# A streaming encoder step on one core: the opening written out by hand for three units at once, without GpSimd arithmetic

## The chip, the cores and the metric

The kernel runs on one core of a Trainium2 chip. Its time is device microseconds of one execution; the median of several runs counts. A core has a matrix engine (PE, with its weight loads shown apart as PEld), a vector engine (DVE), an activation engine (ACT), GpSimd (POOL) and a queue engine (SP), which here issues all transfers. Each works through its own queue in order and waits on semaphores for the others.

## What is computed

One layer of a hybrid encoder, for a prompt of 1024 tokens and a sample of 32:

```python
mod = jax.nn.silu(c) @ p['w_ada'] + p['b_ada']
shift, scale, gate = jnp.split(mod, 3, axis=-1)
hn = rmsnorm(x, p['norm_g']) * (1.0 + scale[:, None]) + shift[:, None]
proj = hn @ p['w_in']
lru_x, lru_g, xbc, z, dt_raw = jnp.split(proj, [...], axis=-1)
...  # RG-LRU on lru_x, gated by lru_g
xbc_c, new_buf_ssd = causal_conv(xbc, buf_ssd, p['ssd_conv_w'], p['ssd_conv_b'])
xs, Bm, Cm = jnp.split(silu(xbc_c), [...], axis=-1)
...  # chunked SSD scan on xs, B, C and dt, gated by z, grouped rmsnorm
mix = jnp.concatenate([y_lru, y_ssd], axis=-1) @ p['w_out']
out = x + gate[:, None] * mix
```

All in float32; the model width is 1024, and w_in has 4624 columns.

## The kernel before

Features lie on the 128 partitions, tokens along the free axis. A *unit* is 128 columns of w_in: a tile of 8 k-tiles of 128x128. 36 units make the input projection; units 24 and 25 are B, 26 and 27 are C, 16 to 23 are xs, 28 to 35 are z, 0 to 15 the LRU part. Tokens come in three blocks (`BLK`): 384, 384 and 290 columns, the last with 256 prompt tokens, 32 sample tokens and 2 columns that hold the shift.

Products are taken in three passes, to keep float32 accuracy: weights and activations are each split into a high part (a cast, on ACT) and a low part (a subtraction), and hi\*hi, hi\*lo and lo\*hi are accumulated (`mm_part`, lines 219 to 221). `load_unit` fetches and splits a unit; the raw, high and low tiles have three buffers each. A unit's product with one block takes one of four PSUM banks tagged "main"; the other four serve everything small.

The shift is not added to the activations. It is multiplied as two extra columns of block 2, and `evacuate` adds the resulting two biases (`shift_bias`) when ACT copies a bank out. So a unit's first two blocks can be copied out only when its third is done.

The opening is the part that this change touches. It must

- load x in three blocks, square it, sum the squares (`load_x`), and from the sums get 1/rms per token (`sum_x`: matmul, root on ACT, reciprocal on DVE), spread it over the partitions by matmul (`spread`), and scale x (`norm_x`);
- multiply 16 units of w_ada with silu(c) (`ada_unit`, line 114; eight for the scale, eight for the shift), copy each row out (line 115), turn it into columns by matmul (`ada_columns`, line 120), and make `Acol` = norm_g * (1 + scale) for each of the 8 k-tiles (`scale_columns`);
- split the scaled x times Acol into `hb` (`h_new`: high part on ACT, line 210, low part on DVE, line 211);
- multiply units 24 and 25 and the dt columns (`dt_block`, line 266) with it.

Inside `tc.manual_schedule` the named engines take their instructions in the order of the program; on the others a planner orders them by simulated time, and it may put later work into gaps. Before, SP and PE are named. Their order comes from two strings, `XLOAD` for the loads and `PROG` for the matmul engine: W is a warm-up matmul on `ones` (line 289), a an ada unit of the scale, s one of the shift, c columns, r and R the sum and scaling of a block of x, p and q one k-tile of unit 24 and 25, d the dt block. GpSimd adds the squares of blocks 1 and 2, scales three k-tiles of block 0 and all of blocks 1 and 2 (line 194, from an SBUF copy of the spread), and makes the low part of unit 24. The opening ends with unit 24's third block; unit 25's third block follows, then units 26 and 27, in the planner's order, with their convolutions (line 419), the dt chain and the SSD loop.

Of the kernel before, what the change touches and what calls it, by code (L numbers as in the profile page):

```python
# [50 lines left out]
def encoder_step(ctx: ExitStack, tc: tile.TileContext, a, o):  # L58
# [98 lines left out]
    xs_in, xsq, xcol, Adone = {}, {}, {}, []  # L157

    def load_x(b, k0, k1):
        c0, n = XB[b]  # L160
# [4 lines left out]
        eng = nc.gpsimd if b else nc.vector
        for k in range(k0, k1, 2):
            tag = "u" if k else ("raw", "zs", "raw")[b]
            sq = cpool.tile([128, 2, 384], F32, name="xsq", tag=tag, bufs=1 if tag == "zs" else 2)[:, :, 0:n]
# [1 line left out]
            nc.scalar.activation(sq, x, AF.Square)  # L170
            if k == 0:
                xsq[b] = sq
            else:
                eng.tensor_add(xsq[b], xsq[b], sq)
        if k1 == KT:
            eng.tensor_add(xsq[b][:, 0, :], xsq[b][:, 0, :], xsq[b][:, 1, :])
# [5 lines left out]
    def norm_x(b):  # L182
        n = XB[b][1]
        bc = spread(xcol[b], n, "xbc")
        sb = cpool.tile([128, 384], F32, name="xbs", tag="raw", bufs=2)[:, 0:n]
        nc.scalar.copy(sb, bc[:, 0:n])
        k = 0
        while k < KT:
            step = 1 if b == 0 else 2
            x = xs_in[b][:, k:k + step, 0:n]  # L190
            if b == 0 and k not in POOL_K:
                nc.vector.tensor_mul(x, x, bc[:, None, 0:n].to_broadcast([128, step, n]))
            else:
                nc.gpsimd.tensor_mul(x, x, sb[:, None, :].to_broadcast([128, step, n]))
            k += step
            ready[b] = k
            h_new()

    ready = [0, 0, 0]
    hdone = [0, 0, 0]  # L200

    def h_new():
        for b in range(3):
            while hdone[b] < min(ready[b], len(Adone)):
                k = hdone[b]
                hdone[b] += 1
                x = xs_in[b][:, k, :]
                for (s, e, w) in [(0, 384, 0)] if b < 2 else [(0, 256, 0), (256, 288, 1)]:
                    hi = hb[b][:, k, 0, s:e]
                    nc.scalar.activation(hi, x[:, s:e], AF.Copy, scale=Acol[:, k, w:w + 1])  # L210
                    nc.vector.scalar_tensor_tensor(hb[b][:, k, 1, s:e], x[:, s:e], Acol[:, k, w:w + 1],  # L211
                                                   hi.bitcast(F32), op0=OP.mult, op1=OP.subtract)
# [59 lines left out]
    with tc.manual_schedule(engines={mybir.EngineType.SP, mybir.EngineType.PE}):  # L272
        dma(cT, a["cT"])
        dma(par, a["par"])
        nc.vector.memset(ones, 1.0)
# [22 lines left out]
        def scale_columns(n):
            k = len(Adone)
            pcol = ada_columns(srow[:, k * 128:(k + n) * 128], n)  # L300
            for i in range(n):
                nc.scalar.activation(Acol[:, k + i, :], pcol[:, i, :], AF.Identity, scale=pc(P_NG, k + i),
                                     bias=b1[:, k + i:k + i + 1])
            Adone.extend(range(k, k + n))
            h_new()

        wB = [None, None]
        sraw = []
        bk = [bk_b0, bk_b1]
        cnt = dict.fromkeys("acrRdpqsW", 0)  # L310
        lcnt = dict.fromkeys("sxwBC", 0)

        def load_next():
            c, n = loads[0], lcnt[loads[0]]
            if c == "s":
                if n >= SR + cnt["a"] + cnt["s"]:
                    return False
                sraw.append(st.tile([128, KT, 128], F32, name="sraw", tag="sraw", bufs=SR))
                dma(sraw[n], a["w_ada"][(n + KT) % (2 * KT)])
            elif c == "x":  # L320
                if n >= XP[0] + XP[1] and cnt["R"] < 1:
                    return False
# [709 lines left out]
```

## Time and profile before

| | |
|---|---|
| median of 3 runs | 786.5 us (785.12 to 788.98) |
| profiled execution | 786.8 us |
| its span, first to last instruction | 785.1 us |
| mean granted clock of PE | 0.987 |
| PE busy | 761.6 us, 97% |
| DVE, ACT, POOL busy | 534.5, 415.2, 78.0 us |
| moved by DMA | 96.32 MB, mean 123 GB/s |

A row of a profile in order of time reads: start in us, duration in us, engine, line, operation, output <- inputs, shapes, count (xN merges N neighbours), and in brackets the idle time of the engine ahead of it and what ended it. In such rows a matmul's duration includes a drain that overlaps the next one, so the distance between starts is its cost in a stream. A row of a stage gives its bounds, its length, and then each engine's busy time with its count, the granted clock, the share of DMA in use and GB/s.

### The profile page before, as it was taken

What the parts mean: (1) busy time and instruction counts of PE and PEld (TensorE: products, weight loads), DVE (VectorE), ACT (ScalarE), POOL (GpSimd) and SP (SyncE); (2) the same over time, 40 slices, a digit from 0 to 9 for tenths busy, and PEclk for the clock granted to TensorE, in tenths of its full rate; (3) what the DMA queues carried; (4) which work ended last, traced back from release to release, by engine and by line L of the source; (5) the groups of instructions that cost most, each with busy time, mean ns of one, the idle gap of its engine ahead of it and who ended that gap; (6) DMA issues with size and microseconds to landing.
All of it is one profiled execution on the core that took longest, in us unless ns stands there. A gap on an engine that the chain in (4) does not pass through costs nothing.

```text
span 785.1 us, 13046 instructions
## 1 busy us (share of the span) xinstructions
PE 761.6 (97%) x5230; PEld 737.0 (94%) x5230; DVE 534.5 (68%) x842; ACT 415.2 (53%) x609; POOL 78.0 (10%) x179
## 2 busy tenths in 40 slices
PE   8899999999999999999999999999999999999994
PEld 7678999989999999998999999999999999999994
DVE  3575966798887787877475566546658897635643
ACT  6553855335244253443578877886777654323430
POOL 3581211001000000000010011101101000000000
PEclk9899999999999999999999999999999999999997
DMA  9920214244433424342212111111153685744831
GB/s 326 395 101 2 78 40 139 88 134 139 137 110 121 147 63 161 116 122 89 78 66 88 43 61 35 54 34 61 31 150 114 191 276 162 236 138 142 262 111 68
DMA packets 40188, 96.32 MB, mean 123 GB/s; under 512 B 4536, under 2 KB 22208, under 8 KB 40128
## 3 DMA queue, kind: packets, MB, share of 16 engines
q1 hardware_dynamic: 40128, 95.50, 37.7%
q8 instruction: 41, 0.67, 0.3%
q14 instruction: 19, 0.16, 0.1%
HBM read 85.53 MB, written 9.95 MB: 122 GB/s over the span
## 4 chain that ended last, share of the span: by engine, by line
PE 80%; DVE 9%; DMA 5%; ACT 2%; issue 2%; POOL 1%; SPq 0%; POOLq 0%; DVEq 0%; ACTq 0%
PE pj L221 16%; PE pj L219 16%; PE pj L220 16%; PE mix L862 6%; PE mix L860 6%; PE mix L861 6%; PE yd L608 2%; PE dS L583 2%; DVE hb L211 2%; DMA M<-dA_d 2%; DVE wlo L97 1%; DMA sraw<-in_w_ada_dram 1%; PE yo L623 1%; DVE M L551 1%; PE gt L744 1%
## 5 line engine op out<-in xcount | busy, mean ns | idle before, releaser
L220 PE MATMUL pj<-hb,whi 128*128 128x384 f32 (+1 forms) x864 | 282.8, 327 | 2.5 <-DVE hb L211 2.5
L219 PE MATMUL pj<-hb,whi 128*128 128x384 f32 (+1 forms) x864 | 284.6, 329 | 0.0
L221 PE MATMUL pj<-hb,wlo 128*128 128x384 f32 (+1 forms) x864 | 282.4, 327 | 1.2 <-POOL wlo L97 1.2
L220 PEld LDWEIGHTS pj<-hb,whi 128*128 128x128 f32 x864 | 163.3, 189 | 4.2 <-DVE hb L211 3.2
L221 PEld LDWEIGHTS pj<-hb,wlo 128*128 128x128 f32 x864 | 163.6, 189 | 3.1 <-POOL wlo L97 1.6
L219 PEld LDWEIGHTS pj<-hb,whi 128*128 128x128 f32 x864 | 162.7, 188 | 3.2 <-issue 2.9
L95 ACT CAST whi<-wraw 128x1024 fp32r<-128x1024 f32 x84 | 88.0, 1048 | 142.3 <-PE pj L220 69.4
L97 DVE TENSOR_TENSOR wlo<-wraw,whi 128x1024 fp32r<-128x1024 f32 x83 | 102.5, 1236 | 59.3 <-ACT whi L95 59.3
L862 PE MATMUL mix<-yt,wlo 128*128 128x324 f32 (+2 forms) x320 | 103.9, 326 | 1.0 <-DVE wlo L97 1.0
L860 PE MATMUL mix<-yt,whi 128*128 128x324 f32 (+2 forms) x320 | 104.1, 325 | 0.0
L861 PE MATMUL mix<-yt,whi 128*128 128x324 f32 (+2 forms) x320 | 103.7, 324 | 0.0
L419 DVE SCALAR_TENSOR_TENSOR u<-raw,par,u 128x1060 f32<-128x1060 f32 x60 | 79.7, 1328 | 1.6 <-ACT u L417 1.1
L862 PEld LDWEIGHTS mix<-yt,wlo 128*128 128x128 f32 x320 | 60.0, 188 | 1.4 <-DVE wlo L97 1.3
L860 PEld LDWEIGHTS mix<-yt,whi 128*128 128x128 f32 x320 | 60.1, 188 | 0.2
L861 PEld LDWEIGHTS mix<-yt,whi 128*128 128x128 f32 x320 | 60.0, 188 | 0.1
L238 ACT ACTIVATE raw<-pj,sb 128x384 f32<-128x384 f32 (+2 forms) x80 | 33.9, 477 | 23.0 <-PE pj L221 13.3
L551 DVE TENSOR_TENSOR_SCAN M<-M,mask 128x1060 f32<-128x1060 f32 x16 | 37.8, 2363 | 11.8 <-DMA M<-dA_d 11.8
L879 DVE SCALAR_TENSOR_TENSOR ot<-mix,gate,xr 128x352 f32<-128x352 f32 (+3 forms) x32 | 14.8, 489 | 25.4 <-PE mix L862 21.5
L405 POOL COPY cso<-raw 128x3 f32<-128x3 f32 x20 | 11.8, 590 | 195.9 <-ACT raw L238 195.9
L211 DVE SCALAR_TENSOR_TENSOR hb<-x,Acol,hb 128x384 fp32r<-128x384 f32 (+2 forms) x32 | 28.0, 925 | 3.8 <-ACT hb L210 3.8
L756 DVE SCALAR_TENSOR_TENSOR r<-a,r 128x1060 f32<-128x1060 f32 x8 | 10.1, 1264 | 28.2 <-ACT r L755 28.2
L554 ACT ACTIVATE M<-M 128x1060 f32<-128x1060 f32 x16 | 17.5, 1091 | 22.2 <-DVE M L551 20.3
(228 smaller groups left out, 1063.5 us busy)
## 6 DMA issues: line engine op xcount, KB each, us to landing
wraw<-in_w_out_dram SPq DMA_DIRECT2D x48, 512.0 KB, 3.6
wraw<-in_w_in_dram SPq DMA_DIRECT2D x36, 512.0 KB, 3.7
M<-dA_d SPq DMA_DIRECT2D x16, 530.0 KB, 4.9
sraw<-in_w_ada_dram SPq DMA_DIRECT2D x16, 512.0 KB, 10.2
E<-E_d SPq DMA_DIRECT2D x16, 265.0 KB, 4.0
yz_d<-y SPq DMA_DIRECT2D x8, 530.0 KB, 4.2
wraw<-in_w_ada_dram SPq DMA_DIRECT2D x8, 512.0 KB, 4.4
x<-in_xh_dram SPq DMA_DIRECT2D x4, 384.0 KB, 4.8
```

The lines of the kernel that those rows point to most:

```text
L95: nc.scalar.copy(hi, raw)
L97: eng.tensor_sub(lo, raw, hi.bitcast(F32))
L211: nc.vector.scalar_tensor_tensor(hb[b][:, k, 1, s:e], x[:, s:e], Acol[:, k, w:w + 1], hi.bitcast(F32), op0=OP.mult, op1=OP.subtract)
L219: nc.tensor.matmul(out, lhsT=hi[:, kk, :], rhs=hh, start=(kk == 0), stop=False)
L220: nc.tensor.matmul(out, lhsT=hi[:, kk, :], rhs=hl, start=False, stop=False)
L221: nc.tensor.matmul(out, lhsT=lo[:, kk, :], rhs=hh, start=False, stop=(kk == KT - 1))
L238: nc.scalar.activation(dst[0:P, off + d:off + d + e - s], banks[b][0:P, s:e], func, bias=sb[0:P, w:w + 1])
L419: nc.vector.scalar_tensor_tensor(u, raw[:, k:k + TW], wcol(k), u, op0=OP.mult, op1=OP.add)
L551: nc.vector.tensor_tensor_scan(M, M, mask, 0.0, op0=OP.add, op1=OP.mult)
L860: nc.tensor.matmul(ps, lhsT=w[0][:, k, :], rhs=yh, start=(half == 1 and k == 0), stop=False)
L861: nc.tensor.matmul(ps, lhsT=w[0][:, k, :], rhs=yl, start=False, stop=False)
L862: nc.tensor.matmul(ps, lhsT=w[1][:, k, :], rhs=yh, start=False, stop=(half == 0 and k == KT - 1))
```

## The change

- PE, SP, ACT, DVE and POOL all follow the written order in the opening; the strings are gone.
- Three units (24, 25, 26) are multiplied k-tile by k-tile: for each k-tile first hi\*hi and lo\*hi of each unit, then hi\*lo of each.
- Loads: x block 0, then w24, s0, w25, s1, s2, w26, s3, s4, x block 1 (halves around s5); each further ada unit is issued after the one whose buffer it takes; x block 2 comes after block 0 is done, in a buffer that it shares with it.
- GpSimd only sets, copies three columns at a time and saves; sums, scalings and weight splits go to DVE. DVE also makes Acol, and ACT copies all ada rows.
- The first two blocks of the three units are copied out without the shift ("parked") into raw tiles, and DVE adds the bias to these 768 columns once block 2 is there.
- Behind the opening, B of group 0 is processed first, then unit 27 is multiplied; dt block 2 stands after block 2 of the units.

```diff
-        eng = nc.gpsimd if b else nc.vector
...
+    def square_x(b, k):
+        n = XB[b][1]
+        if k == 0:
+            xsq[b] = st.tile([128, 2, 384], F32, name="xacc", tag="xacc", bufs=2)[:, :, 0:n]
+        sq = xsq[b] if k == 0 else cpool.tile([128, 2, 384], F32, name="xsq", tag="u", bufs=2)[:, :, 0:n]
+        nc.scalar.activation(sq, xin[b][:, k:k + 2, :], AF.Square)
+        if k:
+            nc.vector.tensor_add(xsq[b], xsq[b], sq)
+        if k == KT - 2:
+            nc.vector.tensor_add(xsq[b][:, 0, :], xsq[b][:, 0, :], xsq[b][:, 1, :])
...
+    def scale_x(b, k, n=1):
+        w = XB[b][1]
+        x = xin[b][:, k:k + n, :]
+        nc.vector.tensor_mul(x, x, xbc[b][:, None, 0:w].to_broadcast([128, n, w]))
...
-    with tc.manual_schedule(engines={mybir.EngineType.SP, mybir.EngineType.PE}):
+    with tc.manual_schedule(engines={E.SP, E.PE, E.Activation, E.DVE, E.Pool}):
...
+        def ada_scale(k):
+            pcol = ada_columns(srow[:, k * 128:(k + 1) * 128], 1)
+            nc.vector.scalar_tensor_tensor(Acol[:, k, :], pcol[:, 0, :], pc(P_NG, k),
+                                           b1[:, k:k + 1].to_broadcast([128, 2]), op0=OP.mult, op1=OP.add)
...
+        def mm_k(us, b, k):
+            for u in us:
+                mm_head(u, b, k)
+            for u in us:
+                mm_tail(u, b, k)
...
+        def park(u, b):
+            if u not in raws:
+                raws[u] = raw_tile(FIRST[u] - 8, ssd_state(FIRST[u] - 16), ("raw", "raw", "zs")[u])
+            for (s, e, d, w) in EV[b]:
+                nc.scalar.copy(raws[u][:, 3 + d:3 + d + e - s], banks[u][b][:, s:e])
...
+        split_w(0)
+        warm(9)
+        sum_x(0)
+        ada_row(0, srow)
+        load_s()
+        warm(3)
+        spread_x(0)
+        ada_scale(0)
+        split_w(1)
+        ada_row(1, srow)
+        load_s()
+        scale_x(0, 0)
+        split_h(0, 0)
...
+        square_x(1, 0)
+        mm_k((2,), 0, 2)
+        mm_k((2,), 0, 3)
+        mm_k((0, 1, 2), 0, 4)
+        ada_row(5, srow)
+        load_s()
+        square_x(1, 2)
+        warm(4)
+        ada_scale(5)
+        split_h(0, 5)
+        square_x(1, 4)
+        mm_k((0, 1, 2), 0, 5)
+        ada_row(6, srow)
+        square_x(1, 6)
+        ada_scale(6)
+        split_h(0, 6)
+        sum_x(1)
+        ada_row(7, srow)
+        spread_x(1)
+        ada_scale(7)
+        split_h(0, 7)
+        scale_x(1, 0, 2)
+        mm_k((0, 1, 2), 0, 6)
+        split_h(1, 0)
+        mm_k((0, 1, 2), 0, 7)
+        load_x(2, 0, 4)
...
+        for k in range(KT):
+            if k % 2 == 0 and k < 6:
+                scale_x(1, k + 2, 2)
+            if k < 6:
+                split_h(1, k + 2)
+            mm_k((0, 1, 2), 1, k)
+            ada_row(KT + k, hrow)
...
+            if k >= 4:
+                square_x(2, 2 * (k - 4))
+        for u in range(3):
+            park(u, 1)
+        dt_block(0)
+        sum_x(2)
+        dt_block(1)
+        spread_x(2)
         pcol = ada_columns(hrow, 8)
         nc.vector.tensor_add(shift, pcol, ...)
...
+        for k in range(0, KT, 2):
+            scale_x(2, k, 2)
+            split_h(2, k)
+            split_h(2, k + 1)
+        for k in range(KT):
+            mm_k((0, 1, 2), 2, k)
+        sbs = []
+        for u in range(3):
+            sbs.append(shift_bias(banks[u]))
+            evacuate(raws[u], 3, AF.Identity, banks[u], 128, (2,), sbs[u])
+            r = raws[u][:, 3:771]
+            nc.vector.tensor_scalar(r, r, sbs[u][:, 0:1], None, op0=OP.add)
+            save_raw(raws[u], FIRST[u] - 8)
         pd = dt_block(2)
...
+    b_post(0, raws[0])
+    banks = project(load_unit(a["w_in"][27]))
+    b_post(1, raws[1])
     dt_chain()
-    for g in range(2):
-        w = load_unit(a["w_in"][26 + g])
-        c_post(g, project(w))
+    c_post(0, raws[2])
+    c_post(1, ssd_raw(banks, 11))
```

More of the change, by code (lines that the diff above doesn't have):

```diff
@@ L156, in encoder_step @@
     XB = ((0, 384), (384, 384), (768, 288))
-    xs_in, xsq, xcol, Adone = {}, {}, {}, []
+    xin, xsq, xcol, xbc = {}, {}, {}, {}
     def load_x(b, k0, k1):
@@ L180, in sum_x, with spread_x, split_h @@
         token_rstd(xcol[b], xsq[b][:, 0, :], XB[b][1], "xcol")
[L182 to L212, printed above, removed]
+    def spread_x(b):
+        xbc[b] = spread(xcol[b], XB[b][1], "xbc")
+    def scale_x(b, k, n=1):
+        w = XB[b][1]
+        x = xin[b][:, k:k + n, :]
+        nc.vector.tensor_mul(x, x, xbc[b][:, None, 0:w].to_broadcast([128, n, w]))
+    def split_h(b, k):
+        x = xin[b][:, k, :]
+        for (s, e, w) in [(0, 384, 0)] if b < 2 else [(0, 256, 0), (256, 288, 1)]:
+            hi = hb[b][:, k, 0, s:e]
+            nc.scalar.activation(hi, x[:, s:e], AF.Copy, scale=Acol[:, k, w:w + 1])
+            nc.vector.scalar_tensor_tensor(hb[b][:, k, 1, s:e], x[:, s:e], Acol[:, k, w:w + 1],
+                                           hi.bitcast(F32), op0=OP.mult, op1=OP.subtract)
     def mm_part(out, w, b, kk):
@@ L292, in encoder_step @@
+        warm(24)
         nc.vector.memset(sc, 0.0)
-        silu = nc.scalar.activation(sc[:, :, 0:2], cT, AF.Silu)
-        with tc.issue_after(silu.ins):
-            nc.scalar.activation(root, eps, AF.Sqrt)
+        nc.scalar.activation(sc[:, :, 0:2], cT, AF.Silu)
+        nc.scalar.activation(root, eps, AF.Sqrt)
         nc.vector.scalar_tensor_tensor(b1, pc(P_BADA, 8, 8), 1.0, pc(P_NG, 0, 8), op0=OP.add, op1=OP.mult)
[L298 to L322, printed above, removed]
-                b = 0 if n < XP[0] else 1 if n < XP[0] + XP[1] else 2
-                i = n - sum(XP[0:b])
-                load_x(b, KT // XP[b] * i, KT // XP[b] * (i + 1))
-            elif c == "w":
-                dma(wdt, a["w_dt"])
+        def ada_row(n, row):
+            ada_unit(sraw[n], row[:, (n % KT) * 128:(n % KT + 1) * 128], nc.scalar.copy)
@@ new lines, in encoder_step @@
+        load_x(2, 0, 4)
+        load_x(2, 4, 8)
+        for i in range(2):
+            load_s()
+        dma(wdt, a["w_dt"])
+        hrow = st.tile([128, D], F32, name="hrow", tag="row", bufs=1)
+        park(0, 0)
+        split_h(1, 1)
+        park(1, 0)
+        park(2, 0)
+        for k in range(KT):
[5 more added lines that the diff above has]
+            ada_row(KT + k, hrow)
+            if len(sraw) < 2 * KT:
+                load_s()
+            if k == 3:
@@ L503, in encoder_step, with b_post @@
     BT = {}
-    def b_post(g, banks, order):
-        u = ssd_conv(ssd_raw(banks, 8 + g, order), 8 + g)
+    def b_post(g, raw):
+        u = ssd_conv(raw, 8 + g)
         bt = tw.tile([128, TW], F32, name="bt", tag="M", bufs=2)
```

160 lines of the change are left out of this document (85 added, 75 removed).

## The prediction

> **What bounds the kernel now.** I read the summary of the page first, then the busy times by stage, then the matmul engine in order of time up to 75 us.
>
> ```profile
> span 785.1 us, 13046 instructions
> PE 761.6 (97%) x5230; PEld 737.0 (94%) x5230; DVE 534.5 (68%) x842; ACT 415.2 (53%) x609; POOL 78.0 (10%) x179
> ...
> 0.00:71.97 71.97, 61.81 (x550) 52.02 (x551) 40.39 (x62) 35.71 (x77) 35.95 (x41) 0.93 0.61 225
> 71.97:75.20 3.23, 3.23 (x26) 3.16 (x24) 1.04 (x3) 0.44 (x2) 0.00 (x0) 1.00 0.00 0
> 75.20:151.00 75.80, 75.80 (x526) 73.67 (x526) 57.79 (x122) 44.95 (x69) 10.96 (x36) 1.00 0.24 74
> ```
>
> The columns of the stage rows are length, then busy time of PE, PEld, DVE, ACT, POOL, then clock and DMA. From 72 to 151 us PE never rests, and over the whole span it is 97% busy. So the time is PE's useful work plus whatever PE wastes, and the opening is where it wastes. Warm-up matmuls count as busy there, so I price useful work by start-to-start distances:
>
> ```profile
> 83.86 0.34 PE L219 MATMUL pj<-hb,whi 128*128 128x384 f32 x1
> ...
> 91.10 0.34 PE L221 MATMUL pj<-hb,wlo 128*128 128x384 f32 x1
> ...
> 71.97 0.30 PE L219 MATMUL pj<-hb,whi 128*128 128x290 f32 x1
> ...
> 75.06 0.29 PE L221 MATMUL pj<-hb,wlo 128*128 128x290 f32 x1
> ...
> 28.41 0.64 PE L114 MATMUL ada_s<-sraw,sc 128*32 128x128 f32 x16
> 28.98 0.44 PE L219 MATMUL pj<-hb,whi 128*128 128x384 f32 x1
> ...
> 39.41 0.81 PE L131 MATMUL xcol<-ones,xsq 128*128 128x1 f32 x6
> ...
> 41.21 0.83 PE L141 MATMUL xbc<-ident,xrs 128*128 128x128 f32 x6
> ...
> 42.94 2.96 PE L266 MATMUL pdt<-hb,wd 128*32 128x384 f32 x16
> ...
> 67.41 1.84 PE L120 MATMUL ada_c<-sel,hrow 128*128 128x2 f32 x16
> ...
> 69.82 2.31 PE L266 MATMUL pdt<-hb,wd 128*32 128x290 f32 x16 [0.57 <-DVE hb L367]
> ```
>
> 42 matmuls of 384 columns start in 7.24 us: 0.177 each; 24 of 290 in 3.09: 0.134. One unit is 16x3x0.177 + 8x3x0.134 = 11.7 us, one k-tile of three units 9x0.177 = 1.6. An ada unit is 0.57. Of the other rows some 0.15 of drain overlaps: dt blocks 2.8, 2.8, 2.15, the shift columns 1.7, a sum 0.62, a spread 0.75. At 75.20 unit 24 is whole (11.7), unit 25 has two blocks (8.5), and there are 16 ada units (9.1), the columns (1.7 + 8x0.14), three sums and spreads (4.1), dt (7.8): 44.0 useful, **31.2 wasted**.
>
> **The change.** It puts five queues in written order and multiplies 24, 25 and 26 together. At T, the end of their third block, PE has 35.1 + 9.1 + 2.8 + 4.1 + 5.6 (two dt blocks) = 56.7 useful behind it. The gain is 31.2 - (T - 56.7), less what comes after. T I get by sending the written order through each queue with these durations:
>
> ```profile
> 5.59 0.83 ACT L170 ACTIVATE xsq<-x 128x768 f32<-128x768 f32 x1
> ...
> 11.50 0.27 ACT L115 COPY srow<-ada_s 128x128 f32<-128x128 f32 x1 [1.52 <-PE ada_s L114]
> ...
> 53.75 1.12 ACT L210 ACTIVATE hb<-x,Acol 128x384 fp32r<-128x384 f32 x2
> ...
> 60.38 1.34 ACT L210 ACTIVATE hb<-x,Acol 128x256 fp32r<-128x256 f32 x4 [0.23 <-POOL x L194]
> ...
> 7.53 0.96 DVE L174 TENSOR_TENSOR xsq<-xsq 128x768 f32<-128x768 f32 x1 [2.95 <-ACT xsq L170]
> ...
> 11.01 0.56 DVE L176 TENSOR_TENSOR xsq<-xsq 128x384 f32<-128x384 f32 x1
> ...
> 17.88 2.40 DVE L192 TENSOR_TENSOR x<-x,xbc 128x384 f32<-128x384 f32 x5
> ...
> 45.15 7.03 DVE L211 SCALAR_TENSOR_TENSOR hb<-x,Acol,hb 128x384 fp32r<-128x384 f32 x4 [2.58 <-ACT hb L210]
> ...
> 52.43 1.13 DVE L211 SCALAR_TENSOR_TENSOR hb<-x,Acol,hb 128x384 fp32r<-128x384 f32 x2
> ...
> 63.71 0.63 DVE L211 SCALAR_TENSOR_TENSOR hb<-x,Acol,hb 128x256 fp32r<-128x256 f32 x2
> ...
> 45.19 6.05 POOL L194 TENSOR_TENSOR x<-x,xbs 128x768 f32<-128x768 f32 x3
> ```
>
> *GpSimd's share goes to DVE.* 45.15 and 45.19 show the price of the old split: while POOL multiplies, a DVE subtraction into hb takes 1.76 us; alone (52.43) 0.57. DVE takes over about 14.6 us (sums of blocks 1 and 2 at 0.96 a step, scalings at 0.48 per 384 columns, one weight split) and gets back 1.2 on each subtraction that ran beside POOL, 4.8 on these four alone. I leave DVE's load in the opening near the 40.4 of its row; its order is what matters. The eight column scalings that go from ACT to DVE, and eight row copies the other way (0.27), stand in the rings below.
>
> *Loads.* Block 0 of x stays first, so its sum is still folded at 11.57. Then come w24, s0, w25, s1, s2, w26 and so on:
>
> ```profile
> 0.00:10.00 10.00, 6.99 (x34) 6.79 (x34) 2.55 (x5) 6.25 (x8) 2.15 (x14) 1.00 0.78 244
> 10.00:20.00 10.00, 9.48 (x100) 8.60 (x101) 4.95 (x9) 6.03 (x13) 4.65 (x4) 0.83 1.04 410
> 20.00:30.00 10.00, 8.35 (x79) 6.53 (x78) 4.54 (x5) 4.89 (x13) 5.11 (x3) 0.83 1.06 383
> ...
> 10.52 0.94 PE L114 MATMUL ada_s<-sraw,sc 128*32 128x128 f32 x16 [2.38 <-DMA sraw<-in_w_ada_dram]
> ```
>
> By these rates and the 1 us by which s0 landed after its bytes, w24 lands at 10.4, s0 12.0, w25 13.4, s2 16.2, w26 17.6, x block 1 at 22.6 and 26.0, s7 at 30, or 31.5 if the scheduler slips later units' loads in front. The ring below wants s7 only at 38, so loads bind only up to w25; each us they are later there moves T by one.
>
> *First product.* Fold 11.57, sum 0.62, root and reciprocal about 0.5, spread, with 0.06 at each hand-off (the ada unit at 10.52 ends at 11.46, its copy starts at 11.50): 14.0. In DVE's order the split of w25 stands before the first scaling and waits for that load: to 15.8, scaling 16.2, hi 16.9. The first projection starts at 16.9.
> *k-tiles 0 to 4:* to 28.9, 12 us for 8.0 of products and 2.3 of ada units.
> *k-tiles 5 to 7:* the ring is ada unit, row copy (ACT), column (PE), Acol (DVE), hi (ACT), product, and the squares and adds of block 1 stand inside it. k=5: ada to 29.5, copy 29.9, square 30.7, add 31.7, Acol 31.9, hi 32.4, product 32.6: PE rests 2.4 us. k=6 likewise: two adds and the fold stand before its Acol, a rest of 2.2. Block 0 ends at 43.3; PE has by then 21 us of work done.
> *Block 1:* 8x(1.6 + 0.57) = 17.3, and 0.6 for a bank that waits for a parked copy: 61.1. ACT and DVE need 1.6 and 1.1 per k-tile there, so PE covers them. The load of x block 2 now waits on SP for the buffer of block 0, that is for its last split (41.5 to 44), and the last four ada weights and dt's queue behind it: x lands at about 48, the last of them at 54, and they are wanted at 54 to 60. That is covered by 2 to 6 us; if it were not, ACT's copy of dt's weights would hold up the hi splits behind it. Parking (six copies) replaces evacuations one for one.
> *dt, sum, dt, spread, shift columns:* 8.7: 69.8. *Block 2:* DVE holds the shift (0.6) before the first scaling (0.66) and hi (0.7): PE rests 2.2. Then scaling, two hi and two lo make a ring of 2.63 per two k-tiles against PE's 2.4: **T = 82.4**. With hand-offs between engines of 0.03 or 0.10 in place of my 0.06: 81.6 and 83.5.
>
> *Clock.* Rests are not free:
>
> ```profile
> 34.42 0.53 PE L220 MATMUL pj<-hb,whi 128*128 128x384 f32 x1 [2.08 <-DVE hb L211]
> 34.75 0.52 PE L221 MATMUL pj<-hb,wlo 128*128 128x384 f32 x1
> ...
> 37.12 1.06 PE L114 MATMUL ada_s<-sraw,sc 128*32 128x128 f32 x16
> 38.11 0.44 PE L219 MATMUL pj<-hb,whi 128*128 128x384 f32 x1
> ...
> 52.41 1.01 PE L141 MATMUL xbc<-ident,xrs 128*128 128x128 f32 x6 [1.66 <-DVE xrs L136]
> ```
>
> After the rest of 2.08 us matmuls start 0.32 apart, 1.81 times the 0.177, until 38; after 1.66 at 52.41 they don't. Three rests of 2.2 to 2.4 each cost up to 3.5 us at that pace, 1.5 lost, part of it absorbed by the rings; with scattered rests between 14 and 24 I take 3.0 (0 to 4.8). T = 85.4, waste 28.7, gain 2.5.
> [...]
>
> *After T.* Units 24 to 26 hold all three weight-split buffers to the end.
>
> ```profile
> 75.27 1.04 ACT L95 CAST whi<-wraw 128x1024 fp32r<-128x1024 f32 x1 [2.65 <-PE pj L220]
> ...
> 76.34 1.23 DVE L97 TENSOR_TENSOR wlo<-wraw,whi 128x1024 fp32r<-128x1024 f32 x1 [0.79 <-ACT whi L95]
> ...
> L419 DVE SCALAR_TENSOR_TENSOR u<-raw,par,u 128x1060 f32<-128x1060 f32 x60 | 79.7, 1328 | 1.6 <-ACT u L417 1.1
> ...
> 146.31 1.02 PE yd L608 x16
> ```
>
> So unit 27's split starts only at T: 1.04 + 1.23 = 2.3, of which dt block 2 covers 2.15; if the evacuations (ACT) and the three new shift additions (DVE, about 0.6 each by their width) go first, 2.5 is left. 0.2 to 2.5; I take 1.3. Before, unit 26 stood ready, so PE had its cover. The three convolutions now arrive at once; I charge 1.0 (0 to 5, rival 2).
>
> Sum: 31.2 - 28.7 - 1.3 - 1.0 = 0.2 gained; slower hand-offs take about 0.7 of it. The profiled execution took 786.8 (span 785.1 and 1.7 around it), 0.3 above the median 786.5: about **787**.
>
> **The rivals.** *1, faster:* rests don't lower the clock: T = 82.4, 784.0; with unit 27's split covered too, and nothing lost behind, 782. For it: full pace at 52.41 after 1.66 of rest; against it 34.42, and these rests are longer than that one. *2, slower:* DVE becomes the bound behind T. Before, 75.20 to the first yd at 146.31 was 71 us for some 54 of DVE work (57.79 to 151) and 17 of waits. Now 12 us of convolutions (nine passes of 1.33) are ready at once, three additions come on top, one split has gone, and PE has 62 us of work (units 27, 16, 17, 28 and 15 of small ones) until it needs yd. Each us by which DVE's 55 and its waits exceed 62 costs one; with 12 of waits it is 5: 792. Against it: the waits shrink when work is piled up, and PE can go on to unit 18. *3, faster:* the squares don't end up inside the ring; block 0 ends by its loads near 35: 778. The written order speaks against it.
>
> **Chances.** Forecast 0.52, rival 1 0.20, rival 2 0.23, rival 3 0.05. The range 781 to 792.5 leaves out rival 3 and the ends of the others. Half a per cent, 3.9 us, is about what a measurement here can tell: below 782.6 lie rival 3, half of rival 1 and a little of the forecast, 0.20; above 790.4 most of rival 2, 0.25.
>
> **What would show it.** First product near 17; block 0 of three units ending at 43 to 47; subtractions into hb of 0.57 throughout; PE rests above 2 us before k-tile 5, the second sum and block 2, with a granted clock under 1 behind them; T at 84 to 87; then a rest of 1 to 2 us before unit 27. An end of block 0 before 40, or PE idle over 4 us between T and 160, would make it wrong.

## The result: 0.8% slower

| | before | changed |
|---|---|---|
| median of 18 runs each | 786.7 us (783.7 to 789.0) | 792.8 us (789.6 to 795.5) |
| ratio to before | | 1.0079, 95% interval 1.0064 to 1.0093 |
| profiled execution, span, clock | 786.8 us, 785.1, 0.987 | 789.6 us, 787.6, 0.991 |
| first yd (start of the SSD loop) | 146.2 us | 156.1 us |

787.0 was forecast, with 781 to 792.5 as the range; 792.8 lies just above it. The changed kernel is 6 us slower, mainly for the reason that rival 2 named, the backlog of DVE behind the opening, though later than rival 2 looked for it. Its profiled execution is the quickest of its 18 runs, 3.2 us under their median; their mean clock is 0.9844.

The head of the changed kernel's page, then its stages (length, busy time of PE, PEld, DVE, ACT, POOL, clock, DMA share, GB/s):

```profile
span 787.6 us, 13027 instructions
PE 761.5 (97%) x5228; PEld 733.1 (93%) x5228; DVE 534.6 (68%) x862; ACT 419.5 (53%) x611; POOL 43.6 (6%) x159
```

```profile
16.66:45.10 28.44, 23.35 (x200) 19.94 (x201) 14.98 (x27) 10.61 (x21) 0.00 (x0) 0.94 0.69 263
45.10:64.50 19.40, 19.13 (x201) 15.06 (x201) 8.85 (x14) 8.69 (x21) 0.00 (x0) 1.00 0.46 167
...
73.50:87.00 13.50, 11.40 (x74) 11.31 (x74) 8.32 (x24) 5.42 (x17) 0.00 (x0) 0.87 0.00 1
87.00:151.00 64.00, 64.00 (x439) 61.98 (x437) 50.15 (x105) 41.83 (x65) 10.85 (x34) 1.00 0.28 82
151.00:175.00 24.00, 21.46 (x156) 19.05 (x154) 19.97 (x39) 9.78 (x13) 0.36 (x2) 1.00 0.40 113
```

POOL is idle from the first product to T (the end of block 2), and PE still rests 5.1 of 28.4 us in block 0 and 2.1 ahead of block 2, both with a clock under 1. Behind T, at 87.0, PE is full to 151 and then rests again. The matmul engine of the changed kernel in order of time:

```profile
16.66 0.45 PE L321 MATMUL pj<-hb,whi 128*128 128x384 f32 x1 [1.21 <-ACT hb L178]
...
29.29 0.64 PE L100 MATMUL ada_s<-sraw,sc 128*32 128x128 f32 x16
...
32.84 0.45 PE L321 MATMUL pj<-hb,whi 128*128 128x384 f32 x1 [1.69 <-ACT hb L178]
...
38.07 0.80 PE L117 MATMUL xcol<-ones,xacc 128*128 128x1 f32 x6 [2.04 <-DVE Acol L310]
...
41.81 0.52 PE L321 MATMUL pj<-hb,wlo 128*128 128x384 f32 x1
...
45.11 0.34 PE L321 MATMUL pj<-hb,whi 128*128 128x384 f32 x1
...
75.66 0.40 PE L321 MATMUL pj<-hb,whi 128*128 128x290 f32 x1 [2.10 <-ACT hb L178]
...
77.52 0.45 PE L321 MATMUL pj<-hb,wlo 128*128 128x290 f32 x1
...
80.25 0.30 PE L321 MATMUL pj<-hb,whi 128*128 128x290 f32 x1
...
86.98 2.29 PE L233 MATMUL pdt<-hb,wd 128*32 128x290 f32 x16
89.11 0.30 PE L187 MATMUL pj<-hb,whi 128*128 128x290 f32 x1
...
153.04 1.57 PE L661 MATMUL dS<-xw,B_tm 128*128 128x128 f32 x10 [0.94 <-DVE xw L647]
...
169.60 0.63 PE L645 MATMUL xsT<-ident,u 128*128 128x128 f32 x4 [0.39 <-DVE y L705]
...
173.28 0.27 PE L645 MATMUL xsT<-ident,u 128*32 128x128 f32 x1 [1.21 <-DVE y L705]
```

The first product, the three rests and the half-pace matmuls behind two of them (0.52 for 0.34, 0.45 for 0.30) stand where the prediction put them. The last three rows belong to the new loss: PE waits for DVE in the first iterations of the SSD loop.

To see where time is lost I take out of the traces, for the same amount of useful PE work done (at full pace, each kind of matmul at its closest spacing, which is less than the prediction's prices for the small ones), the time spent beyond that work. The sizes depend on the prices chosen; only differences between the columns are used:

| useful work done, us | before | changed | two_at_once | before_dve_opening | columns_ahead |
|---|---|---|---|---|---|
| 20 | 33.0 | 28.3 | 33.8 | 26.7 | 26.1 |
| 50 (T of the changed kernel) | 38.0 | 36.8 | 39.6 | 33.8 | 32.5 |
| 200 | 54.0 | 56.9 | 56.6 | 49.6 | 54.0 |
| 700 (end) | 71.8 | 74.9 | 73.2 | 67.2 | 71.5 |

At 50 us of work the changed kernel is ahead by 1.2 us; from there to 200 it loses 4.1 more than the kernel before (20.1 against 16.0), and behind that little changes. The other columns belong to the experiments.

### The profile page after: what moved, and what is told of

Same layout as the page of the kernel before. It is cut to its first block, busy times and chain, and to the rows that moved or that the text cites. A ratio compares the mean times of both kernels' runs of the same rounds, so it can differ in the third digit from the quotient of the medians.

```text
span 787.6 us, 13027 instructions
## 1 busy us (share of the span) xinstructions
PE 761.5 (97%) x5228; PEld 733.1 (93%) x5228; DVE 534.6 (68%) x862; ACT 419.5 (53%) x611; POOL 43.6 (6%) x159
## 4 chain that ended last, share of the span: by engine, by line
PE 76%; DVE 11%; DMA 5%; ACT 4%; issue 2%; SPq 0%; POOL 0%; POOLq 0%; DVEq 0%; ACTq 0%
PE pj L187 13%; PE pj L188 13%; PE pj L189 13%; PE mix L940 6%; PE mix L938 6%; PE mix L939 6%; PE pj L321 3%; DMA M<-dA_d 3%; PE yd L686 2%; PE dS L661 2%; PE pj L325 2%; DVE wlo L83 1%; DVE u L497 1%; PE ada_s L100 1%; DVE M L629 1%
## 5 line engine op out<-in xcount | busy, mean ns | idle before, releaser
L188 PE MATMUL pj<-hb,whi 128*128 128x384 f32 (+1 forms) x792 | 259.5, 328 | 0.0
L187 PE MATMUL pj<-hb,whi 128*128 128x384 f32 (+1 forms) x792 | 259.4, 328 | 0.0
L189 PE MATMUL pj<-hb,wlo 128*128 128x384 f32 (+1 forms) x792 | 258.9, 327 | 0.0
L189 PEld LDWEIGHTS pj<-hb,wlo 128*128 128x128 f32 x792 | 149.4, 189 | 2.0 <-issue 1.5
L188 PEld LDWEIGHTS pj<-hb,whi 128*128 128x128 f32 x792 | 149.3, 189 | 1.4 <-issue 1.3
L187 PEld LDWEIGHTS pj<-hb,whi 128*128 128x128 f32 x792 | 148.8, 188 | 1.5 <-issue 1.2
L206 ACT ACTIVATE raw<-pj,sb 128x256 f32<-128x256 f32 (+1 forms) x74 | 30.7, 468 | 36.5 <-PE pj L189 24.1
L321 PE MATMUL pj<-hb,whi 128*128 128x384 f32 (+1 forms) x72 | 25.9, 365 | 5.8 <-ACT hb L178 5.4
L670 DVE SCALAR_TENSOR_TENSOR dS<-dS,dec_bc 128x64 f32<-128x64 f32 x128 | 26.6, 268 | 3.3 <-ACT dS L665 2.7
```

The source lines that it names most:

```text
L187: nc.tensor.matmul(out, lhsT=hi[:, kk, :], rhs=hh, start=(kk == 0), stop=False)
L188: nc.tensor.matmul(out, lhsT=hi[:, kk, :], rhs=hl, start=False, stop=False)
L189: nc.tensor.matmul(out, lhsT=lo[:, kk, :], rhs=hh, start=False, stop=(kk == KT - 1))
L206: nc.scalar.activation(dst[0:P, off + d:off + d + e - s], banks[b][0:P, s:e], func, bias=sb[0:P, w:w + 1])
L321: nc.tensor.matmul(banks[u][b], lhsT=ws[u][i][:, k, :], rhs=hb[b][:, k, 0, :], start=(k == 0 and i == 0), stop=False)
```

## The experiments

Three theories. **A**, rival 2: three units at once pile up DVE's convolutions at T and take away unit 26's product, under which they ran before. **B**: the rests of the opening are paid twice, by the half pace behind them. **C**: the written order makes every k-tile of block 0 pass a chain (ada unit, row copy, column, Acol, high part) with the squares of block 1 inside it, and this eats what GpSimd's removal gives. All runs in one table; "work" is the mean of span times granted clock, "clock" of span times the rest. That is no exact split, since half pace costs nothing where PE would have waited, but it tells the two kinds of loss apart. About 4 to 5 us of each "clock" are the end of the span, where the clock is 0.50 and PE has next to nothing to do: in the profiled executions from 779.76 us on in the changed kernel (PE busy for 0.40 of 7.84 us) and from 775.31 on in the kernel before (1.77 of 9.79). The first yd is that of the profiled execution.

| kernel | median us (lowest to highest, runs) | ratio to before (95%) | work | clock | first yd |
|---|---|---|---|---|---|
| before | 786.7 (783.7 to 789.0, 18) | | 773.7 | 11.4 | 146.2 |
| changed | 792.8 (789.6 to 795.5, 18) | 1.0079 (1.0064, 1.0093) | 778.4 | 12.3 | 156.1 |
| changed_two_taps_less | 786.3 (784.7 to 794.5, 12) | 1.0020 (0.9996, 1.0044) | 774.1 | 11.6 | 146.0 |
| before_two_taps_less | 785.8 (783.5 to 786.9, 12) | 0.9994 (0.9980, 1.0008) | 772.2 | 11.7 | 146.7 |
| two_at_once | 790.6 (787.0 to 791.8, 12) | 1.0051 (1.0036, 1.0067) | 774.2 | 13.7 | 149.7 |
| lambda_late | 792.5 (788.5 to 794.8, 7) | 1.0066 (1.0042, 1.0091) | 779.3 | 10.6 | 156.2 |
| warm_rests | 786.4 (783.7 to 788.4, 12) | 0.9989 (0.9975, 1.0003) | 778.1 | 6.0 | 155.0 |
| before_warm | 781.2 (780.0 to 785.6, 12) | 0.9943 (0.9926, 0.9960) | 773.5 | 6.2 | 144.1 |
| warm_two_taps_less | 784.1 (782.5 to 786.4, 12) | 0.9976 (0.9962, 0.9990) | 776.3 | 6.3 | 144.0 |
| before_dve_opening | 781.1 (777.3 to 783.9, 8) | 0.9932 (0.9907, 0.9956) | 768.4 | 10.3 | 142.0 |
| squares_out | 795.3 (791.8 to 797.4, 6) | 1.0107 (1.0084, 1.0131) | 778.0 | 15.1 | 158.9 |
| planner_order | 795.9 (795.3 to 797.7, 4) | 1.0118 (1.0100, 1.0137) | 780.3 | 13.9 | 162.9 |
| columns_ahead | 785.8 (783.4 to 790.1, 12) | 0.9998 (0.9981, 1.0015) | 774.8 | 9.2 | 152.9 |
| dve_opening_warm | 780.5 (778.5 to 781.1, 6) | 0.9925 (0.9905, 0.9944) | 771.0 | 7.4 | 142.8 |
| dve_opening_warm_columns | 779.1 (778.4 to 780.1, 5) | 0.9913 (0.9893, 0.9933) | 772.3 | 5.1 | 141.6 |
| dve_opening_columns | 776.6 (775.6 to 777.5, 5) | 0.9873 (0.9854, 0.9893) | 769.7 | 5.1 | 139.0 |

The kernel before was measured with each set of runs: it stood at 786.2 to 786.8 in the other sets, with 773.7 to 774.2 of work and 10.3 to 11.4 of clock. Work and clock in its row are those of the set with 786.8. Differences between kernels are taken from the ratios, a thousandth being 0.79 us.

### A: the backlog behind T

**Two taps less**, in the changed kernel and, as control, in the kernel before. Two of the three DVE passes in the convolutions of units 24 to 27 are left out, so these convolutions lack two of their terms.

```diff
-        for k in range(3):
+        for k in range(taps):
...
-        return conv(raw, lambda k: pc(P_SCW, 12 * k + t), pc(P_SCB, t))
+        return conv(raw, lambda k: pc(P_SCW, 12 * k + t), pc(P_SCB, t), 3 if t < 8 else 1)
```

> The changed kernel with two of the three DVE passes left out of the convolutions of units 24 to 27 (B and C only): 8 x 1.31 = 10.5 us less DVE work between the opening's end and the first yd, all else the same. Theory DVE backlog: the first yd comes 6 to 10 us before 156, the rests of PE between 98 and 257 us (4.8 in sum) fall below 2, and the time falls by 2.5 to 4 us from 792.8. Rival (those rests come from how the planner placed the transposes and states in PE's order, not from DVE's load): within 1 us.

> The control: the same two passes left out of the same convolutions of the kernel before. Theory DVE backlog: there PE has the products of units 26 and 27 as cover, and its rests between 98 and 254 us are 1.7 in sum: the time falls by 0 to 1.2 us from 786.8. If it falls as much as the changed kernel's, the load of DVE isn't what the change made worse.

The changed kernel gets 4.6 us back (1.0079 to 1.0020), its first yd moves from 156.1 to 146.0, and its work is that of the kernel before. The kernel before does not move beyond its interval. The stages from 87 to 160 and from there to 257, first in the kernel before, then in the changed kernel, then in the changed kernel with two taps less:

```profile
87.00:160.00 73.00, 72.28 (x508) 69.88 (x507) 53.38 (x115) 36.95 (x55) 6.43 (x24) 1.00 0.26 83
160.00:257.00 97.00, 96.40 (x732) 92.28 (x736) 81.43 (x143) 40.79 (x55) 6.37 (x21) 1.00 0.41 129
```

```profile
87.00:160.00 73.00, 72.06 (x492) 68.39 (x491) 59.15 (x127) 46.26 (x71) 11.21 (x36) 1.00 0.29 83
160.00:257.00 97.00, 94.70 (x724) 88.77 (x722) 85.55 (x152) 44.22 (x55) 4.52 (x19) 1.00 0.45 137
```

```profile
87.00:160.00 73.00, 73.00 (x518) 69.15 (x518) 53.49 (x128) 44.38 (x69) 11.15 (x34) 1.00 0.30 89
160.00:257.00 97.00, 97.00 (x726) 92.72 (x726) 83.01 (x142) 40.83 (x54) 6.64 (x21) 1.00 0.41 132
```

The changed kernel's rests of PE, 0.94 and 2.30 us, are gone. So DVE's backlog costs the changed kernel 4 to 5 us (the two intervals together leave some 2.4 to 6.8), and costs the kernel before nothing that can be measured. The rests themselves are 3.2 us against 1.3 in the kernel before, 1.9 more, so not quite half of the 4.1 lost from 50 to 200 us of work can be seen as rests; where the other half lies is not shown.

**Two units at once.** The convolutions stay; unit 26 goes back behind the opening, with its load, split and product.

```diff
-FIRST = (24, 25, 26)
+FIRST = (24, 25)
...
-    banks = project(load_unit(a["w_in"][27]))
...
-    c_post(0, raws[2])
-    c_post(1, ssd_raw(banks, 11))
+    for g in range(2):
+        w = load_unit(a["w_in"][26 + g])
+        c_post(g, ssd_raw(project(w), 10 + g))
```

> Edit: the changed kernel with two units (24 and 25) in the opening instead of three; unit 26's load, split and product go back behind the opening, where the kernel before has them. Theory A (the third unit's product, moved ahead of T, is the cover that VectorE's convolutions lack behind T): the rests between T and 257 us shrink (4.8 us of rests in the changed kernel against 1.7 in the kernel before), the first yd comes within about 147 to 150 us instead of 156.1, and up to 4.6 us come back (what two taps less gave); against it the products of the opening are a third shorter, so that what VectorE does for each k-tile is less covered and the opening wastes 2 to 5 us more. Together 789 to 793. Theory B (the loss lies in the new order of the opening and not in the cover behind it): the first yd stays late by the same amount against the useful work done, and the time is 793 to 798.

Theory A's outcome: 790.6, with the first yd at 149.7. Work falls by 4.2 to that of the kernel before. The loss from 50 to 200 us of useful work is 17.0 (56.6 - 39.6), against 20.1 with three units and 16.0 before. The opening pays 2.8 for it (39.6 against 36.8), as two units cover less of each k-tile. Only 2.2 us of time come of the 4.2 of work, as the clock column is 1.4 worse (13.7 against 12.3). What three units gain ahead of T they lose, and a little more, behind it.

**The small DVE chain late.** In the program, the one-off DVE operations on Lambda, which stand between T and the first yd, go into the third iteration of the SSD loop.

```diff
+        if j == 2:
+            lam_chain()
```

> The changed kernel with the LRU's softplus constants (some 25 DVE operations of 8 columns, 0.16 us each, interleaved with the dt chain) computed in the SSD loop at j = 2 rather than behind the opening. Theory DVE backlog: DVE has 4 us less to do between T and the first yd; yd comes 3 to 4 us before 156, PE rests less than 2.5 us between 151 and 175, the time falls by 1.5 to 4 us. Theory clock: no change of the time beyond 1 us.

No change (1.0066 against 1.0079, first yd 156.2), but this settles nothing: behind the opening the planner orders DVE, and it put these operations where they had been. On the tile `lamn` they start from 100.5 to 127.3 us, in the changed kernel from 99.9 to 126.6. So the run is in effect the changed kernel once more, and whether the chain is in the way stays untested.

### B: the clock

**Warm-up matmuls in the rests.** In the changed kernel 4, 6 and 7 ahead of the first product, k-tile 5 and the second sum, and 7 in a bank of their own ahead of block 2; in the kernel before 8, 5 and 7 more W in `PROG`.

```diff
+        warm(4)
...
+        warm(6)
...
+        warm(7)
...
+        wb = pbank([128, 128], "warm")
+        for i in range(7):
+            nc.tensor.matmul(wb, lhsT=ones[:, 0:128], rhs=ones[:, 0:128], start=True, stop=True)
```

> The changed kernel with warm-up matmuls put into four rests of PE in the opening: 4 ahead of the first product, 6 more ahead of k-tile 5, 7 ahead of the second sum, 7 ahead of block 2 (in a bank of their own). Nothing else moves. Theory clock (the profiled execution, at a granted clock of 0.991, is among the fastest; the timed ones have 0.979 to 0.989, so most executions lose one to five more windows of 3.4 us at half pace to the rests): the granted clock rises to 0.99 or more in nearly all executions, the median falls from 792.8 by 3 to 5 us to 788 to 790, and the spread of 6 us halves. Rival DVE backlog (what is lost is lost behind the opening, where DVE is the bound): within 1 us of 792.8.

> The kernel before with 20 more warm-up matmuls in three of its rests of PE: 8 ahead of the first ada unit (rest of 2.38 us), 5 ahead of the products between which the rest of 1.24 falls, 7 ahead of the product that ends the rest of 2.08. Theory clock (a rest of 1.2 to 2.4 us makes the next 3.4 us half as fast, in this kernel too: its timed clock is 0.9855, no better than the changed kernel's 0.9845): clock 0.991 or more, the time falls by 2 to 4 us to 783 to 785, so the clock loss is about the same in both kernels and isn't what separates them. Rival (the clock loss is what the change added, the kernel before loses little): within 1 us of 786.8.

The changed kernel gains 7.1 us, and nearly all of it is clock (12.3 to 6.0; work 778.4 and 778.1). But the kernel before gains 4.5 in the same way. So half pace costs both kernels about as much: it is a loss that the prediction rightly counted on both sides, and at most 2.6 us of what separates them. The filled rests of the changed kernel, and two half-pace stretches that were left:

```profile
33.31 0.45 PE L321 MATMUL pj<-hb,whi 128*128 128x384 f32 x1 [0.25 <-ACT hb L178]
...
70.70 1.95 PE L106 MATMUL ada_c<-sel,hrow 128*128 128x2 f32 x16
72.51 2.31 PE L451 MATMUL warm<-ones 128*128 128x128 f32 x14
...
75.16 0.45 PE L321 MATMUL pj<-hb,wlo 128*128 128x290 f32 x1
...
94.39 2.11 PE L472 MATMUL dtT<-selD,dtp 32*128 32x16 f32 x18
...
99.23 0.52 PE L189 MATMUL pj<-hb,wlo 128*128 128x384 f32 x1
...
101.25 0.34 PE L187 MATMUL pj<-hb,whi 128*128 128x384 f32 x1
```

No rest stands ahead of 75.16 or 99.23, yet the matmuls there run at half pace. By the distances between starts the first stretch sets in at 73.7, among the warm-ups, and the second at 97.5; what precedes both is a row of tiny matmuls, 16 of 2 columns and 18 of 16 columns. Such a row does not always have this effect: in the changed kernel the same 18 stand at 95.82, and the clock is 1.00 throughout behind them. The last section sets both beside the times at which the clock changes.

**Both losses taken away** (the warm-ups, and the two passes left out as above):

> Edit: the changed kernel with the warm-up products of warm_rests and with two of three passes left out in the convolutions of units 24 to 27 (as in changed_two_taps_less). If the clock's loss ahead of T (6.4 us) and VectorE's backlog behind it (4.6 us) are two separate losses: 781 to 783, ratio 0.993 to 0.996. Rival (they are one loss, counted twice: products at half pace shift the same rests): 785 to 787, no quicker than either alone.

0.9976, between the two: 8.1 us gained where 7.1 and 4.6 would make 11.7. The clock's part is there nearly in full (6.3 are left, against 6.0 with the warm-ups alone), of the backlog's 4.3 of work only 2.1 is. The two overlap, and why by that much stays open.

### C: where GpSimd's removal went

**That part alone**, in the kernel before: its order, with GpSimd's arithmetic on DVE.

```diff
-        eng = nc.gpsimd if b else nc.vector
+        eng = nc.vector
...
-            if b == 0 and k not in POOL_K:
+            if True:
...
-                wB[i] = split_unit(fetch_unit(a["w_in"][24 + i]), eng=(nc.gpsimd, nc.vector)[i])
+                wB[i] = split_unit(fetch_unit(a["w_in"][24 + i]), eng=nc.vector)
```

> One part of the change alone: the kernel before with GpSimd's additions, scalings and its weight split given to DVE, order and loads as before. DVE takes over some 20 us of work (36 us of POOL's at its own pace) and gets back 1.2 us on each of some 12 subtractions. If GpSimd's arithmetic cost more than it saved, the rests of 1.24 (POOL wlo) and 2.08 (DVE hb) shrink and the time falls by 1 to 3 us; if DVE's order now puts more ahead of hb, within 2 us of 786.8 or slower by up to 3.

5.3 us faster, more than the 1 to 3 expected, and all of it is work (773.8 to 768.4). The subtraction into hb, by groups of the first 90 us (count, busy us, mean ns; idle before), in the kernel before, this one and the changed one:

```profile
L211 DVE SCALAR_TENSOR_TENSOR hb<-x,Acol,hb 128x384 fp32r<-128x384 f32 x16 | 21.0, 1358 | 3.8 <-ACT hb L210 3.8
```

```profile
L211 DVE SCALAR_TENSOR_TENSOR hb<-x,Acol,hb 128x384 fp32r<-128x384 f32 x16 | 9.0, 611 | 1.3 <-ACT hb L210 1.3
```

```profile
L179 DVE SCALAR_TENSOR_TENSOR hb<-x,Acol,hb 128x384 fp32r<-128x384 f32 x16 | 9.9, 619 | 12.1 <-ACT hb L178 12.1
```

DVE takes over GpSimd's arithmetic and gets 12.0 us back on these sixteen instructions. In the kernel before, ten of the sixteen run while a TENSOR_TENSOR of GpSimd runs, and they take 0.97 to 2.71 us, 1.81 in the mean; the other six take 0.60 to 0.61, about the mean that all sixteen have without GpSimd's arithmetic (0.61, and 0.62 in the changed kernel). So a subtraction beside GpSimd's arithmetic took three times as long; by what it is held up is not shown. How much of the 5.3 us comes by these subtractions, and how much by waits on GpSimd that are gone, is not shown. The third row shows that the changed kernel has this gain too, but its DVE then waits 12.1 us for ACT's high part: this points to the order, not the engine, as its limit.

**The squares moved out of the chain.** In the changed kernel each square of block 1 goes behind the Acol and the split that it delayed, and the second sum behind block 0, covered by four ada units of the shift. The edit also drops the four warm-ups behind ada unit 5.

```diff
-        sum_x(1)
...
         mm_k((0, 1, 2), 0, 7)
+        ada_row(8, hrow)
+        ada_row(9, hrow)
+        sum_x(1)
+        ada_row(10, hrow)
+        spread_x(1)
+        ada_row(11, hrow)
```

> The changed kernel with the squares and sums of x block 1 taken out of the ring of k-tiles 5 to 7 (each stands behind the Acol and the split that it delayed; four ada units of the shift are moved between block 0 and block 1 to cover the second sum). Theory ring: the rests ahead of k-tile 5 (1.69 us) and ahead of the second sum (2.04 us) go, a shorter one comes ahead of block 1; block 0 ends 3 to 5 us sooner than 45.1, the opening's end T near 83 in place of 87, the time 3 to 6 us less than 792.8 and the clock higher. Rival DVE backlog: T is earlier, but DVE's work starts earlier with it, so the gain stays; if instead DVE's total work to the first yd were the bound from time 0, yd would stay at 156 and the time within 1 us.

A miss: 795.3. The work stays (778.0 against 778.4), and what is lost is clock (15.1 against 12.3). Without the squares each product waits 0.96 us for its own column and high part, and block 1 now waits for its scaling and for the three parked copies that ACT takes ahead of its high part:

```profile
32.05 0.44 PE L321 MATMUL pj<-hb,whi 128*128 128x384 f32 x1 [0.96 <-ACT hb L178]
...
37.48 0.45 PE L321 MATMUL pj<-hb,whi 128*128 128x384 f32 x1 [0.96 <-ACT hb L178]
...
41.64 0.44 PE L321 MATMUL pj<-hb,whi 128*128 128x384 f32 x1 [0.96 <-ACT hb L178]
...
49.37 0.44 PE L321 MATMUL pj<-hb,whi 128*128 128x384 f32 x1 [2.04 <-ACT hb L178]
```

So it is the chain itself, not the squares, that cannot be covered by the product before it.

**The planner's order on ACT, DVE and POOL:**

```diff
-    with tc.manual_schedule(engines={E.SP, E.PE, E.Activation, E.DVE, E.Pool}):
+    with tc.manual_schedule(engines={E.SP, E.PE}):
```

> The changed kernel with only SP and PE in written order, as in the kernel before; ACT, DVE and POOL are ordered by the planner. Theory ring (the order written for ACT and DVE puts squares ahead of the columns): the planner may take the columns first; 2 to 4 us less. Rival: PE's written order has the same waits, so the order on DVE and ACT matters little: within 2 us of 792.8.

3 us slower than the written order (1.0118), which neither theory nor rival expected. Waits of PE in its first 100 us (in total, times, longest), the first of which is 5.4 in the changed kernel:

```profile
PE pj L321 <- ACT hb L178: 6.8, 4, 3.5
PE pj L325 <- DVE hb L179: 3.8, 2, 2.8
```

**The chain run ahead.** Rows, columns and Acol of k-tiles 5 to 7 are made behind k-tile 4, the squares stand between them, and four ada units of the shift cover block 1's scaling.

```diff
-        square_x(1, 2)
-        warm(4)
+        ada_row(6, srow)
         ada_scale(5)
         split_h(0, 5)
+        square_x(1, 2)
+        ada_row(7, srow)
+        ada_scale(6)
+        ada_scale(7)
         square_x(1, 4)
+        split_h(0, 6)
         mm_k((0, 1, 2), 0, 5)
-        ada_row(6, srow)
         square_x(1, 6)
-        ada_scale(6)
-        split_h(0, 6)
-        sum_x(1)
-        ada_row(7, srow)
-        spread_x(1)
-        ada_scale(7)
         split_h(0, 7)
-        scale_x(1, 0, 2)
         mm_k((0, 1, 2), 0, 6)
-        split_h(1, 0)
+        sum_x(1)
         mm_k((0, 1, 2), 0, 7)
+        spread_x(1)
...
+        for k in range(4):
+            ada_row(8 + k, hrow)
...
+        scale_x(1, 0, 2)
```

> Edit: the changed kernel, with the ada rows, columns and Acol of k-tiles 5, 6 and 7 made right behind k-tile 4, ahead of the products of k-tile 5; the squares of block 1 stand between them, the second sum stands behind the product of k-tile 6 and its spread behind that of k-tile 7; four ada units of the shift stand ahead of block 1 as cover, and four fewer in it. Theory (the chain of ada unit, row copy, column, Acol and high part, with the squares inside, is what holds block 0 up): the rests of 1.69 and 2.04 us and half of the half-pace stretch behind them go, block 0 ends near 39 to 40 instead of 45.1, with 1.7 us of ada units done that stood in block 1; T near 82 to 84 instead of 87.0, and the time 787 to 790. Rival (VectorE's squares and splits bound block 0 whatever the order, so the rests only move to other places): T at 86 to 88 and 792 to 795.

```profile
32.91 0.38 PE L106 MATMUL ada_c<-sel,srow 128*128 128x2 f32 x2 [0.96 <-ACT srow L101]
...
40.18 0.83 PE L127 MATMUL xbc<-ident,xrs 128*128 128x128 f32 x6
40.94 1.95 PE L100 MATMUL ada_s<-sraw,sc 128*32 128x128 f32 x64
44.55 0.44 PE L321 MATMUL pj<-hb,whi 128*128 128x384 f32 x1 [1.66 <-ACT hb L178]
...
82.66 2.29 PE L233 MATMUL pdt<-hb,wd 128*32 128x290 f32 x16
```

Block 0 ends at 40.2 instead of 45.1, T is 82.7 instead of 87.0, and the ratio goes from 1.0079 to 0.9998: 6.4 us, a little more than theory C asked for, 3.6 in work and 3.1 in clock. The order of a few instructions was worth as much as the whole measured loss. The backlog stays (21.5 lost from 50 to 200 us of useful work), so the kernel ends level with the one before.

**The better version.** Since GpSimd's removal alone gains, I put the other findings on the kernel before: the warm-ups, then the shift's 16 tiny matmuls two by two among the large ones, then the 12 warm-ups in the middle taken out again.

```diff
-PROG = ("WWWWWWWWWaWWWWWWraWRWcWaWWWWWWcWWWWqpaWWWaqcaqWp"
+PROG = ("WWWWWWWWWWWWWWWWWaWWWWWWraWRWcWaWWWWWWcWWWWqpaWWWaqcaqWp"
...
+                if cols < cnt["s"] and last != "s":
+                    column()
+            last = c
+        while cols < 8:
+            column()
-        pcol = ada_columns(hrow, 8)
```

> Edit: the kernel before with the opening's GpSimd arithmetic on VectorE (as in before_dve_opening) and with the warm-up products of before_warm. If the two gains are apart (5.3 us by the one, 4.5 to 5 us by the other): 776 to 778, ratio about 0.988, granted clock about 0.99. Rival (the quicker opening has rests in other places, so that the same warm-up products fill none of them or stand in the way): 780 to 782, clock 0.986 as without them.

> Edit: as dve_opening_warm, and the 16 tiny products of the shift's columns are put one pair at a time among the large products, instead of 16 in a row. Theory (a stretch of tiny products counts as a rest for the clock): the half-pace stretch that follows them goes, 0 to 1.7 us less than dve_opening_warm in the mean, clock higher by up to 0.002. Rival (tiny products count as work): the same as dve_opening_warm within 0.5 us, or up to 1 us slower, as each column then waits for its row ahead of a product.

> Edit: as dve_opening_warm_columns, without the 12 added warm-up products in the middle of the opening (5 ahead of a k-tile, 7 ahead of the second spread); the 8 added ones at the start stay. Theory (those 12 fill no rest in the quicker opening and stand in the way): 775 to 778, with the clock no more than 0.003 lower. Rival (they hold the clock up and cost nothing): 779 to 782.

With 20 warm-ups 780.5: clock 2.9 better, work 2.6 worse, which is the rival's time, though not its clock. With the columns spread out 779.1; the intervals overlap, so that difference alone is suggested and not shown, and the traces leave it open too. First dve_opening_warm, then dve_opening_warm_columns:

```profile
62.41 1.84 PE L120 MATMUL ada_c<-sel,hrow 128*128 128x2 f32 x16
64.82 3.44 PE L266 MATMUL pdt<-hb,wd 128*32 128x290 f32 x16 [0.57 <-DVE hb L367]
```

```profile
63.88 0.72 PE L343 MATMUL ada_c<-sel,hrow 128*128 128x2 f32 x6
65.17 2.33 PE L266 MATMUL pdt<-hb,wd 128*32 128x290 f32 x16 [0.57 <-DVE hb L380]
```

The same 16 matmuls take 3.44 us behind a row of tiny ones and 2.33 without. But in the kernel before they take 2.31 behind the same unbroken row (67.41 and 69.82 in the prediction), so this pair alone doesn't show that the spreading removed the slow stretch. The mean clock loss of the runs, 7.4 against 5.1, points that way. Without the 12 warm-ups 776.6, at 0.9873 the fastest of all, as the theory that they fill no rest had it. It is 10 us faster than before and 16 faster than the change.

## Why the prediction was wrong

*What held.* First product 16.9 (16.66); end of k-tile 4 28.9 (29.3); the rests ahead of k-tile 5, the second sum and block 2 2.4, 2.2 and 2.2 (1.69, 2.04, 2.10); subtractions of 0.57 throughout (0.62); a clock under 1 behind the rests (0.50 behind those of 2.04 and 2.10, though 1.00 behind that of 1.69); loads and dt's weights covered. PE never waits for a transfer in the opening.

*T, mis-sized by 1.6.* 85.4 was forecast, 86.98 came; blocks 0 and 2 took about what was summed for them with the 3.0 charged for the clock. Two terms were short: block 1 took 19.4 us (the stage row) where 17.9 was summed, since alternating between ada units and products costs 2.36 per k-tile, not 2.17; dt, sums and columns took 9.06 instead of 8.7. With the prediction's 56.7 of useful work at T, the waste is 30.3 and the gain 0.9 instead of 2.5; the table above has 1.2.

*Unit 27's split, charged at 1.3, cost nothing.* Its first product (89.11) follows dt block 2 (86.98, 2.29 long) without a rest. The casts went ahead of the evacuations on ACT. That this cancels most of the 1.6 is luck.

*The failing step: "The three convolutions now arrive at once; I charge 1.0."* The term was too small by 3 to 4 us: they cost 4 to 5, which is 4.1 by the trace, 4.6 by two taps less, 4.2 of work by two units at once. Rival 2 had the mechanism and nearly the price (5, 792) and got 0.23. What argued against it, "PE can go on to unit 18", did happen: PE is busy 64.00 of 64 us from 87 to 151 while the first yd slips by 10 us. But going on only defers the debt. The products taken early are missing as cover in the first SSD iterations, where PE then waits for DVE at 153.04, 169.60 and 173.28. I had looked for the loss between T and the first yd, and most of it lies behind that.

*The clock* was charged at 3.0 and stands in both kernels: in the means of all runs 4.7 us of the difference are work (778.4 against 773.7) and 0.9 clock (12.3 against 11.4). Rival 1, rests without loss of clock, is refuted: with the rests filled and the work unchanged the kernel gains 7.1 us. Rival 3 gave block 0 an end near 35 if the squares left the chain; taken out, they made it worse. It named the wrong link, though the chain was worth 6.4 us.

*The profile and the median.* In the profiled executions the loss is 2.8 us (789.6 against 786.8), of which the steps above explain 4.1 - 1.2. The other 3.2 is its distance from the median of its kernel: it had a higher clock than most runs (0.991 against a mean of 0.9844).

*Still open* is why GpSimd's removal in the old order beats the repaired new order: before_dve_opening needs 768.4 of work, columns_ahead 774.8. At 50 us of work the new order is even ahead (32.5 against 33.8); the 5.7 behind it (21.5 against 15.8, one half-pace stretch in it) fit the backlog, but three units at once with a cover for their convolutions was not tried.

## What to carry to other kernels

Work that is moved ahead of a stage is no longer there to cover the stage: before three products are put into one place, ask what the next engine was doing underneath them, and follow its backlog until it is paid off, not only to the next milestone. In a chain of small steps over several engines, start the next round's small steps ahead of the large product, and measure each part of a rewrite by itself: here one part alone gained 5.3 us and the rest of the rewrite more than spent it.
